# A state space stage in a two-layer trunk: response matrices on SyncE's queue, and half of the output projection in seven products

## The chip, the core and the metric

The kernel runs on one core of one Trainium2 chip. The core has five engines with instruction streams of their own: TensorE (PE, matrix products into PSUM; PEld is its weight load), VectorE (DVE), ScalarE (ACT), GpSimd (POOL) and SyncE (SP, which here only issues DMAs). Sixteen DMA engines move data between HBM and SBUF for all of them. The metric is the device time of one execution in microseconds (us); lower is better.

## What is computed

The reference is a trunk of two layers on 256 tokens of width 2048, all in float32: layer 0 mixes tokens with a gated MLP, layer 1 with a state space layer; each then has a cross-attention over 256 memory rows and a squared-ReLU MLP. The change lies in the state space layer, whose reference is, cut to its core:

```python
def s5_glu(h, w_in, lam_re, lam_im, log_dt, bm_re, bm_im, cm_re, cm_im, d_skip, w_out, b_out):
    u = (h @ w_in).astype(F32).reshape(bsz, seq, B_GROUPS, B_GROUP)
    ...
    _, states = lax.associative_scan(combine, (a, bu), axis=0)
    y = jnp.einsum('gcp,sbgp->bsgc', cmat, states).real + d_skip.astype(F32) * u
    y = jax.nn.gelu(y.reshape(bsz, seq, B_WIDTH), approximate=False).astype(h.dtype)
    val, gate = jnp.split(y @ w_out + b_out, 2, axis=-1)
    return val * jax.nn.sigmoid(gate)
```

There are 128 groups of 16 channels with 64 complex states each. `w_in` is 2048 x 2048, `w_out` 2048 x 4096.

## The kernel before

**Products in float32.** PE multiplies a reduced form of float32. Every operand is therefore split into a high part (a cast, on ACT, L103) and a low part (source minus high part, on DVE, L104), and a product is high x high, low x high and high x low. A weight tile is 128 x 1024 (two k tiles of 128 rows by 512 columns, 512 KB). SP loads it (`wload`, L117 to L128, four raw buffers), `wtile` splits it (three buffers of each part), and `gemm_tok` (L141) lets PE run 12 matmuls on it: two k tiles, two halves of the tokens, three parts. After each weight tile `tick` (L83) counts one step, and `at(delay, fn)` (L78) plans other work so many steps later: this is how the small steps of the state space stage are laid between weight tiles.

**The order of instructions.** The program is traced in this order, and a scheduler at build time keeps an order by priority for each engine, in which an instruction can come later than it was traced when its buffer is not yet free. `issue_after(ins)` forces what is issued in its block behind `ins` on the same engine. `self.fed` is the last weight load. SP's DMAs are issued in order; a DMA that waits for its buffer holds up what follows it on SP.

**Seven products.** `gemm_seven` (L784) computes two column chunks at once. On the first 4 of 16 k tiles it treats tokens (two halves), k (two blocks of two k tiles) and the two chunks as 2 x 2 blocks and forms the product with seven block products instead of eight (a Winograd form). For this it takes sums of the left operand, made once (`token_sums`, L748), and differences of the raw weight tiles, made on DVE (L856, L862, L869, L876). Each block product is a split and six matmuls. The other 12 k tiles run as direct weight tiles (`direct`, L831). Four raw tiles are loaded by `fetch` (L796). Column chunks are `n0` and `n0 + 1`. Partial sums are handed to `gather`, the last ones to `end`. It runs in the attention (values, output projection) and in the second MLP.

**The state space stage** (`s5`, L1259). It has four chunks n of 32 groups. `gemm_tok` on `b_w_in` gives the chunk's inputs (8 weight tiles, so 8 steps); `follow(n)` (L1412) then plans the chunk's own steps: `inputs` (transposes), `own` (products with pq), `states`, `carry` (the recurrence on DVE), `outputs` in two halves (steps 14 and 16, with exceptions in the last chunks; L1384 multiplies with the response matrix dq, L1392 with qq), `activated` (Gelu) and `features`. Behind the four chunks stands the output projection `b_w_out`, value chunks 0 to 3 and gate chunks 4 to 7 of 512 columns, 8 weight tiles each; j = 0 begins before the last chunk's outputs are done and runs over chunks 0, 1 and 4 in turns.

**Where dq, pq and qq come from.** They were written to HBM earlier (Pd, Qd, Kd). `fetch` (L1281) loads them for a chunk, four of each:
- pq, 512 KB, on POOL's queue, four buffers;
- qq, 512 KB, on SP's queue behind `self.fed` (`stream=True`), four buffers;
- dq, the response matrix, into four fixed tiles `resp` (L1276) of 128 x 1024, lower block triangular: four pieces of 32 rows with 256, 512, 768 and 1024 values in a row (32, 64, 96 and 128 KB), on POOL's queue. The source of a piece is the pattern `[[P, 2], [(2 * T - 1) * P, 16], [1, 2 * (h + 1) * P]]` (L1293): 2 by 16 rows. A piece for chunk n can land only when the outputs of chunk n - 1 have read the tile.

`load` (L1269) chooses the queue. In `follow`, dq of a chunk n > 0 is planned at steps 7 and 9 (8 and 10 for the last chunk), qq at 10 and 12 (11 and 13), two at a time; for chunk 0 dq is issued at the start and qq at steps 2, 4, 6 and 8. The preparation of the stage during the first MLP loads lb with SP, whose sources have the patterns [8][16][512] (L1165, L1166).

**Closing of a chunk pair** (L1467 to L1483): value and gate accumulators get their bias (loaded on POOL), sigmoid on ACT, product, residual add, all on 128 x 1024, and one step later the next norm's chunk.

Of the kernel before, what the change touches and what calls it, by code (L numbers as in the profile page):

```python
# [9 lines left out]
F32 = mybir.dt.float32  # L10
F32R = mybir.dt.float32r
I32 = mybir.dt.int32
AF = mybir.ActivationFunctionType
ALU = mybir.AluOpType
AX = mybir.AxisListType

P = 128
D = 2048
S = 256
KT = D // P  # L20
NB = 512
NCH = D // NB
KB = 2
# [15 lines left out]
class Trunk:  # L39
# [741 lines left out]
                    made.add(k)  # L781
        return raw, t1, t2, load, add

    def gemm_seven(self, tiles, token, sums, w, n0, k0, gather, end=None, own=None, ahead=None, then=None, raw=None):  # L784

# [2 lines left out]
        nc = self.nc  # L790
        v = nc.vector
        kc0 = k0 // KB
        ws, run, kept = tiles
        raw, half = raw or {}, lambda t: t.rearrange("p (k c) -> p k c", k=KB)

        def fetch(i, j):  # L796
            t = ws()
            self.fed = nc.sync.dma_start(out=half(t), in_=w[n0 + j, kc0 + i]).ins
            raw[i, j] = t

        def parts(src, own=None):
# [6 lines left out]
        def into(key, kts, left, hi, lo):  # L808
            out = banks[key]
            mm = lambda s, m, e: nc.tensor.matmul(out, s, m, start=key not in begun, stop=e, skip_group_check=True)  # L810
            for kk in kts:
                ah, al = left(kk)
                mm(ah, hi[:, kk, :], False)
                begun.add(key)
                mm(al, hi[:, kk, :], False)
            for kk in kts:
                mm(left(kk)[0], lo[:, kk, :], True)
# [13 lines left out]
        def direct(j, first):  # L831

            kc = todo[j].pop(0)
            hi, lo = self.wtile(w, n0 + j, kc0 + kc)
            for t in (first, 1 - first):
                into((t, j), range(KB), lambda kk: token(KB * kc + kk, t), hi, lo)
                yield
            self.tick()

        def whole(*a):  # L840
            for _ in direct(*a):
                pass
# [8 lines left out]
        for i, j in ((0, 0), (0, 1), (1, 0), (1, 1)):  # L851
            if (i, j) not in raw:
                fetch(i, j)
        run = run()
# [32 lines left out]
        while len(todo[0]) > 1 or len(todo[1]) > 1:  # L887
            j = len(todo[1]) > len(todo[0])
# [370 lines left out]
    def s5(self, x, cur, nxt):  # L1259
        nc, a, tc = self.nc, self.a, self.tc  # L1260
        hT = cur.act
        NQ = G // NCH
        with tc.tile_pool(name="s5", bufs=2, reuse_waits="tile") as sp:
            yT = self.new_act()
            st = {}

            ahead = {}

            def load(src, out, stream=False):  # L1269
                if stream:  # L1270
                    with tc.issue_after(self.fed):
                        nc.sync.dma_start(out=out, in_=src)
                else:
                    nc.gpsimd.dma_start(out=out, in_=src)

            resp = [sp.tile([P, T * P], F32, name=f"dq{i}", bufs=1) for i in range(4)]  # L1276
# [4 lines left out]
            def fetch(nm, n, i, stream=False):  # L1281


                if nm == "pq":
                    t = sp.tile([P, 2, 4, P], F32, name=nm, bufs=4)
                    load(self.Pd[4 * n + i], t, stream)
                elif nm == "qq":
                    t = sp.tile([P, 2, 4 * P], F32, name=nm, bufs=4)
                    load(self.Qd[4 * n + i].rearrange("l p r n -> (l p) r n"), t, stream)
                else:  # L1290
                    t, kd = resp[i], self.Kd[4 * n + i]
                    for h in range(4):
                        load(bass.AP(tensor=kd.tensor, offset=kd.offset + 6 * P,  # L1293
                                     ap=[[P, 2], [(2 * T - 1) * P, 16], [1, 2 * (h + 1) * P]]),
                             t[32 * h:32 * h + 32, 2 * (3 - h) * P:])
                ahead[nm, n, i] = t

            def chunks(n, acc):
# [17 lines left out]
            def inputs(n):  # L1316
                u = st[n].pop()
                us = sp.tile([P, 8, 4, NC], F32, name="us")
                st[n] += [us]
                for h in range(2):  # L1320
                    pt = self.ps([P, 4, P])
                    for l in range(4):
                        nc.tensor.transpose(pt[:, l, :], u[:, 4 * h + l].rearrange("p j c -> p (j c)"), self.ident)
                    nc.scalar.copy(out=us[:, 4 * h:4 * h + 4].rearrange("p l t c -> p l (t c)"), in_=pt)
# [87 lines left out]
            def follow(n):  # L1412

                late = n == NCH - 1
                self.at(5 + late, lambda: own(n))
                for i in range(4):
                    if n + 1 < NCH:
                        self.at(5, lambda i=i: fetch("pq", n + 1, i))
                    if n:
                        self.at(7 + late + i // 2 * 2, lambda i=i: fetch("dq", n, i))  # L1420
                        self.at(10 + late + i // 2 * 2, lambda i=i: fetch("qq", n, i, True))
                self.at(4 + late, lambda: inputs(n))
                self.at(6 + late, lambda: states(n))
                self.at(7 + late, lambda: [carry(n, 2, 15), carry(n, 4, 7, 2)])
                self.at(8 + late, lambda: [carry(n, c, 1, 4) for c in (8, 12, 16)])
                self.at(9 + late, lambda: [carry(n, c, 1, 4) for c in (20, 24, 28)])
                self.at(10 + late, lambda: [carry(n, 6, 7, 2), carry(n, 3, 15)])
                gap = n == NCH - 2
                self.at(14 + 1.5 * gap, lambda: outputs(n, 0))
                self.at(16 + gap, lambda: outputs(n, 1))  # L1430
                self.at(16 + gap, lambda: activated(n))
                self.at(17 + gap if n >= NCH - 2 else 19, lambda: features(n))

            for i in range(4):
                fetch("pq", 0, i)
            for i in range(4):
                fetch("dq", 0, i)
                self.at(2 * i + 2, lambda i=i: fetch("qq", 0, i, True))
            for n in range(NCH):
                acc = self.gemm_tok(hT, a["b_w_in"], n)  # L1440
                if n == 0:
# [1 line left out]
                chunks(n, acc)  # L1443
                follow(n)

            nxt.start()
            wo = a["b_w_out"]
            for j in range(NCH):
                if j == 0:
                    spare = self.psM.pop()  # L1450
                    av1 = [spare.tile([P, NB], F32, name="ps") for _ in range(2)]
                    part = lambda n, acc, k: self.gemm_tok(yT, wo, n, acc=acc, kts=range(*k), first=k[0] == 0,
                                                           last=k[1] == KT)
                    av, _, ag = (part(n, acc, (0, 4)) for n, acc in ((0, None), (1, av1), (NCH, None)))
                    for k in (4, 8):
                        for n, acc in ((0, av), (1, av1), (NCH, ag)):
                            part(n, acc, (k, k + 4))
                    self.flush()
                    for n, acc in ((0, av), (NCH, ag)):
                        part(n, acc, (12, KT))  # L1460
                elif j == 1:
                    av = part(1, av1, (12, KT))
                    ag = self.gemm_tok(yT, wo, NCH + 1)
                else:
                    av = self.gemm_tok(yT, wo, j)
                    ag = self.gemm_tok(yT, wo, NCH + j)
                cs = slice(j * NB, (j + 1) * NB)  # L1467
                bv = self.bc(sp, a["b_b_out"][j * NB:(j + 1) * NB])
                bg = self.bc(sp, a["b_b_out"][D + j * NB:D + (j + 1) * NB])
                val = sp.tile([P, 2, NB], F32, name="val", tag="pq", bufs=4)  # L1470
                gat = sp.tile([P, 2, NB], F32, name="gat", tag="pq", bufs=4)
                b2 = lambda b: b.unsqueeze(1).broadcast_to([P, 2, NB])
                if j == 1:
                    for t in range(2):
                        nc.vector.tensor_tensor(out=val[:, t], in0=av1[t], in1=bv, op=ALU.add)
                    self.psM.append(spare)
                else:
                    nc.vector.tensor_tensor(out=val, in0=av, in1=b2(bv), op=ALU.add)
                nc.vector.tensor_tensor(out=gat, in0=ag, in1=b2(bg), op=ALU.add)
                nc.scalar.activation(out=gat, in_=gat, func=AF.Sigmoid)  # L1480
                nc.vector.tensor_tensor(out=val, in0=val, in1=gat, op=ALU.mult)
                nc.vector.tensor_tensor(out=x[:, :, cs], in0=x[:, :, cs], in1=val, op=ALU.add)
                self.at(1, lambda j=j: nxt.chunk(x, j))  # L1483
# [185 lines left out]
```

## Time and profile before

| | |
|---|---|
| median of 3 runs | 2770.2 us (2769.85 to 2771.99) |
| profiled execution | 2772.35 us, span of its instructions 2770.2 us |
| mean granted TensorE clock | 0.999 |
| PE busy | 99% of the span, 14966 matmuls |
| DVE, ACT, POOL busy | 75%, 51%, 7% |
| state space stage | about 1385 us to 1694 us after the span's start |

The profile is one execution. Busy time of PE counts matmuls, which are pipelined, so a matmul's duration is longer than its distance to the next one. A row of the timeline has the start, the duration, engine, line, operation, output and inputs, and in brackets the idle time before it and what ended it. A row of the waits has who waited for whom, then total us, times, longest. A row of the DMA issues has the queue's engine, the count, KB of one and the median time from issue to landing. A row of the table by stretches has the stretch, its length, busy time and count of instructions for PE, PEld, DVE, ACT and POOL, then granted clock, busy share of the 16 DMA engines and GB/s.

### The profile page before, as it was taken

Reading aid. Unit: us, or ns where it says so; the run is one execution under the profiler, and the core shown is the slowest. Engines: PE = TensorE matmul, PEld = TensorE weight load, DVE = VectorE, ACT = ScalarE, POOL = GpSimd, SP = SyncE. Lnnn points to the kernel's source line nnn. Section 1 sums busy time; section 2 is a strip of 40 time slices with the busy share of each in tenths; the row PEclk is TensorE's granted clock in tenths of the full one; section 3 lists DMA queues with packets and bytes.
Section 4 is the critical chain, followed back from the end, with each engine's and each line's share of the span. In section 5 each row is a group of like instructions: output and inputs, shape, how many; then the busy total and the mean of one; then the engine's idle time right before and its main releaser. Section 6 shows DMA issues by size and latency. Waiting matters only on the chain. (4 is left out here: it accounts for less than half of the span.)

```text
span 2770.2 us, 39500 instructions
## 1 busy us (share of the span) xinstructions
PE 2748.3 (99%) x14966; PEld 2325.4 (84%) x14966; DVE 2066.9 (75%) x2835; ACT 1426.7 (51%) x1822; POOL 184.9 (7%) x331
## 2 busy tenths in 40 slices
PE   9999999999999999999999999999999999999998
PEld 7888888888888888888888788888888888888887
DVE  6865757878888878787577657568767978879685
ACT  5545545655544434444566445446555655546454
POOL 0100000001011111111203100000000000000000
PEclk9999999999999999999999999999999999999999
DMA  8766566457688887886879766564556557575565
GB/s 293 231 199 214 189 193 217 152 160 238 211 281 259 262 258 257 265 259 219 235 239 284 207 203 206 188 213 156 181 165 231 180 171 241 158 246 166 176 212 160
DMA packets 194175, 593.75 MB, mean 214 GB/s; under 512 B 44096, under 2 KB 45168, under 8 KB 193472
## 3 DMA queue, kind: packets, MB, share of 16 engines
q1 hardware_dynamic: 153456, 537.46, 61.1%
q0 software_dynamic: 40000, 52.71, 6.6%
q8 instruction: 117, 1.92, 0.3%
q10 hardware_dynamic: 528, 1.06, 0.1%
q14 instruction: 74, 0.61, 0.1%
HBM read 567.51 MB, written 23.46 MB: 213 GB/s over the span
## 5 line engine op out<-in xcount | busy, mean ns | idle before, releaser
L104 DVE TENSOR_TENSOR wlo<-wraw,whi 128x1024 fp32r<-128x1024 f32 (+1 forms) x857 | 1041.0, 1220 | 434.8 <-ACT whi L103 429.0
L103 ACT CAST whi<-wraw 128x1024 fp32r<-128x1024 f32 (+1 forms) x857 | 899.4, 1051 | 800.2 <-PE acc L910 172.1
L174 PE MATMUL acc<-act,whi 128*128 128x512 f32 x3072 | 740.9, 391 | 0.6 <-DVE act L246 0.6
L174 PEld LDWEIGHTS acc<-act,whi 128*128 128x128 f32 x3072 | 563.1, 188 | 110.6 <-issue 1.4
L179 PEld LDWEIGHTS acc<-act,wlo 128*128 128x128 f32 x3072 | 395.0, 191 | 17.4 <-DVE wlo L104 1.8
L179 PE MATMUL acc<-act,wlo 128*128 128x256 f32 x3072 | 403.3, 283 | 1.3 <-DVE wlo L104 1.0
L159 PE MATMUL acc<-whi,act 128*128 128x512 f32 x1472 | 370.4, 393 | 5.6 <-ACT whi L103 5.5
L159 PEld LDWEIGHTS acc<-whi,act 128*128 128x128 f32 x1472 | 275.2, 189 | 63.6 <-ACT whi L103 6.3
L810 PE MATMUL acc<-whi,act 128*128 128x512 f32 x824 | 222.7, 392 | 0.0
L910 PE MATMUL acc<-whi,hl 128*128 128x512 f32 x544 | 212.7, 391 | 0.0
L909 PE MATMUL acc<-whi,hh 128*128 128x512 f32 x544 | 212.6, 391 | 0.0
L159 PE MATMUL acc<-wlo,act 128*128 128x512 f32 x736 | 197.9, 391 | 0.0
L810 PEld LDWEIGHTS acc<-whi,act 128*128 128x128 f32 x824 | 152.9, 188 | 35.9 <-ACT ends L846 2.2
L159 PEld LDWEIGHTS acc<-wlo,act 128*128 128x128 f32 x736 | 138.6, 188 | 28.9
L912 PE MATMUL acc<-wlo,hh 128*128 128x512 f32 x544 | 145.8, 389 | 0.0
L810 PE MATMUL acc<-wlo,act 128*128 128x512 f32 x412 | 127.2, 391 | 0.2
L190 ACT COPY r<-acc 128x512 f32<-128x512 f32 x64 | 37.6, 587 | 161.9 <-PE acc L174 161.9
L910 PEld LDWEIGHTS acc<-whi,hl 128*128 128x128 f32 x544 | 102.1, 188 | 22.2 <-issue 1.0
L810 PE MATMUL acc<-whi,hh 128*128 128x512 f32 x308 | 120.5, 391 | 0.0
L909 PEld LDWEIGHTS acc<-whi,hh 128*128 128x128 f32 x544 | 102.1, 188 | 21.4 <-issue 0.2
L912 PEld LDWEIGHTS acc<-wlo,hh 128*128 128x128 f32 x544 | 102.0, 188 | 21.4 <-issue 0.2
L810 PE MATMUL acc<-whi,hl 128*128 128x512 f32 x308 | 119.9, 389 | 0.0
(387 smaller groups left out, 2951.3 us busy)
## 6 DMA issues: line engine op xcount, KB each, us to landing
wraw<-in_f_w_up SPq DMA_DIRECT2D x256, 512.0 KB, 4.5
wraw<-in_f_w_down SPq DMA_DIRECT2D x200, 512.0 KB, 5.6
wraw<-in_x_w_q SPq DMA_DIRECT2D x64, 512.0 KB, 3.7
wraw<-in_x_w_k SPq DMA_DIRECT2D x64, 512.0 KB, 4.5
wraw<-in_b_w_out SPq DMA_DIRECT2D x64, 512.0 KB, 4.5
wraw<-in_a_w_in SPq DMA_DIRECT2D x63, 512.0 KB, 4.7
wraw<-in_x_w_o SPq DMA_DIRECT2D x48, 512.0 KB, 4.3
wraw<-in_x_w_v SPq DMA_DIRECT2D x40, 512.0 KB, 3.9
```

Source lines behind the costliest of these rows:

```text
L103: self.nc.scalar.copy(out=hi, in_=src)
L104: return self.nc.vector.tensor_tensor(out=lo, in0=src, in1=hi.bitcast(F32), op=ALU.subtract).ins
L159: nc.tensor.matmul(out[t], a[:, kt, sl], b[:, kk, :], start=st and a is ah, stop=en)
L174: nc.tensor.matmul(acc[:, f, :], hi[:, kk, sl], both[:, kt].rearrange("p a s -> p (a s)"), start=first and kk == 0, stop=last and kk == FK ...
L179: nc.tensor.matmul(acc[:, f, 0:S], lo[:, kk, sl], ah[:, kt, :], start=False, stop=last and kk == FK - 1, skip_group_check=True)
L190: nc.scalar.copy(out=dst, in_=acc[:, :, S:])
L810: mm = lambda s, m, e: nc.tensor.matmul(out, s, m, start=key not in begun, stop=e, skip_group_check=True)
L909: nc.tensor.matmul(acc[:, t, :], ah, hi[:, kk, :], start=kt == 0, stop=False)
L910: nc.tensor.matmul(acc[:, t, :], al, hi[:, kk, :], start=False, stop=False)
L912: nc.tensor.matmul(acc[:, t, :], hid[kt // 4][0][:, kt % 4, sl], lo[:, kk, :], start=False, stop=kt == KT - 1)
```

## The change

1. `load` takes the queue for dq too, and dq is loaded on SP's queue behind `self.fed`, with its steps moved: for chunk 0 at steps 6, 8, 14 and 16 (qq three steps after each), for the others at 12, 12, 14 and 14, and qq one step after. Pieces and tiles stay as they are.
2. Value chunks 2 and 3 run with their gate chunks 6 and 7 through `gemm_seven`, with a distance `step=NCH` between the two column chunks. The sums of yT are made once, three steps into j = 1. Raw tiles live in the four `resp` tiles, the kept partial sums in tiles of the stage that are free by then.
3. With `step > 1`, `fetch` in `gemm_seven` issues the raw tiles behind the last weight load.
4. The closing of these two pairs runs by halves of the tokens: bias adds, sigmoid, product and residual add on 128 x 512.

```diff
-    def gemm_seven(self, tiles, token, sums, w, n0, k0, gather, end=None, own=None, ahead=None, then=None, raw=None):
+    def gemm_seven(self, tiles, token, sums, w, n0, k0, gather, end=None, own=None, step=1, ahead=None, then=None, raw=None):
...
             t = ws()
-            self.fed = nc.sync.dma_start(out=half(t), in_=w[n0 + j, kc0 + i]).ins
+            with self.tc.issue_after(self.fed) if step > 1 else nullcontext():
+                self.fed = nc.sync.dma_start(out=half(t), in_=w[n0 + step * j, kc0 + i]).ins
             raw[i, j] = t
...
-            hi, lo = self.wtile(w, n0 + j, kc0 + kc)
+            hi, lo = self.wtile(w, n0 + step * j, kc0 + kc)
...
                     for h in range(4):
-                        load(bass.AP(tensor=kd.tensor, offset=kd.offset + 6 * P,
+                        load(stream=stream, src=bass.AP(tensor=kd.tensor, offset=kd.offset + 6 * P,
                                      ap=[[P, 2], [(2 * T - 1) * P, 16], [1, 2 * (h + 1) * P]]),
-                             t[32 * h:32 * h + 32, 2 * (3 - h) * P:])
+                             out=t[32 * h:32 * h + 32, 2 * (3 - h) * P:])
...
-                    if n:
-                        self.at(7 + late + i // 2 * 2, lambda i=i: fetch("dq", n, i))
-                        self.at(10 + late + i // 2 * 2, lambda i=i: fetch("qq", n, i, True))
+                for k, nm in enumerate(("dq", "qq")) if n else ():
+                    for i in range(4):
+                        self.at(12 + i // 2 * 2 + k, lambda nm=nm, i=i: fetch(nm, n, i, True))
...
-            for i in range(4):
-                fetch("dq", 0, i)
-                self.at(2 * i + 2, lambda i=i: fetch("qq", 0, i, True))
+            for k, nm in enumerate(("dq", "qq")):
+                for i in range(4):
+                    self.at((6, 8, 14, 16)[i] + 3 * k, lambda nm=nm, i=i: fetch(nm, 0, i, True))
...
+            def block_sums():
+                y = sp.tile([P, 4, S], F32, name="ysum", tag="qq", bufs=4)
+                nc.vector.tensor_tensor(out=y, in0=yT[0][:, 0:4].bitcast(F32), in1=yT[1][:, 0:4].bitcast(F32), op=ALU.add)
+                sums.append(self.token_sums(sp.tile([P, KB * NB], F32, name="s", tag="qq", bufs=4),
+                                            lambda: sp.tile([P, 4, 2, P], F32R, name="sums", tag="us"),
+                                            y[:, 0:2], y[:, 2:4]))
+
+            def gated_pair(j):
+
+                cs = slice(j * NB, (j + 1) * NB)
+                bias = [self.bc(sp, a["b_b_out"][o + j * NB:o + (j + 1) * NB]) for o in (0, D)]
+                val = sp.tile([P, 2, NB], F32, name="val", tag="pq", bufs=4)
+                gat = sp.tile([P, 2, NB], F32, name="gat", tag="pq", bufs=4)
+                held, done = {}, set()
+                v = nc.vector
+
+                def part(t, n, p):
+                    v.tensor_tensor(out=p, in0=p, in1=bias[n - j], op=ALU.add)
+                    held[t, n - j] = p
+
+                def end(t, n, src):
+                    out = (val, gat)[n - j][:, t]
+                    v.tensor_tensor(out=out, in0=src, in1=held.get((t, n - j), bias[n - j]), op=ALU.add)
+                    if n > j:
+                        nc.scalar.activation(out=out, in_=out, func=AF.Sigmoid)
+                    done.add((t, n - j))
+                    if (t, 0) in done and (t, 1) in done:
+                        v.tensor_tensor(out=val[:, t], in0=val[:, t], in1=gat[:, t], op=ALU.mult)
+                        v.tensor_tensor(out=x[:, t, cs], in0=x[:, t, cs], in1=val[:, t], op=ALU.add)
+
+                run = sp.tile([P, KB * NB], F32, name="run", tag="u", bufs=1)
+                keep = [sp.tile([P, 2, NB], F32, name="keep", tag="vv") for _ in range(2)]
+                homes = iter(resp)
+                self.gemm_seven((lambda: next(homes), lambda: run, lambda i: keep[i // 2][:, i % 2]),
+                                lambda kt, t: [f[:, kt, t * P:(t + 1) * P] for f in yT[:2]],
+                                sums, wo, j, 0, part, end, step=NCH)
...
+            sums = []
             for j in range(NCH):
+                if j == 1:
+                    self.at(3, block_sums)
+                if j >= 2:
+                    gated_pair(j)
+                    self.at(1, lambda j=j: nxt.chunk(x, j))
+                    continue
```

More of the change, by code (lines that the diff above doesn't have):

```diff
@@ L1460, in s5 @@
                         part(n, acc, (12, KT))
-                elif j == 1:
+                else:
                     av = part(1, av1, (12, KT))
                     ag = self.gemm_tok(yT, wo, NCH + 1)
-                else:
-                    av = self.gemm_tok(yT, wo, j)
-                    ag = self.gemm_tok(yT, wo, NCH + j)
                 cs = slice(j * NB, (j + 1) * NB)
```

## The prediction

> **What bounds the kernel now.** I read the page first, then the PE's waits, then the state space stage on PE, POOL and SyncE (SP), then the DMA issues. On the page (the row of q1, the queue of SP, has packets, MB moved and the share of 16 engines' span) and in the list of PE's waits:
>
> ```profile
> span 2770.2 us, 39500 instructions
> PE 2748.3 (99%) x14966; PEld 2325.4 (84%) x14966; DVE 2066.9 (75%) x2835; ACT 1426.7 (51%) x1822; POOL 184.9 (7%) x331
> q1 hardware_dynamic: 153456, 537.46, 61.1%
> ```
> ```profile
> PE acc L159 <- ACT whi L103: 5.5, 1, 5.5
> PE ps L1384 <- DMA dq<-Kd: 2.5, 2, 1.9
> PE ps L1337 <- ACT us L1324: 1.7, 2, 0.9
> ```
>
> PE is busy 99% of the span, and its few waits add up to about 12 us. So there are two ways to gain: fewer matmuls, or the 2.5 us that the last chunk's outputs wait for response matrices. There is more room to lose: whatever starves PE of split weight tiles goes straight into the time. The stage on PE, first the start of the first half of the outputs of chunks 0 and 3, then the two halves of chunk 3 with the tiles beside them:
>
> ```profile
> 1453.38 1.08 PE L1384 MATMUL ps<-dq,us 128*32 128x128 f32 x32
> ...
> 1545.07 1.07 PE L159 MATMUL acc<-wlo,act 128*128 128x512 f32 x4
> 1546.06 1.08 PE L1384 MATMUL ps<-dq,us 128*32 128x128 f32 x32
> ...
> 1551.07 1.98 PE L159 MATMUL ps<-whi,act 128*128 128x512 f32 x8
> 1552.88 1.07 PE L159 MATMUL ps<-wlo,act 128*128 128x512 f32 x4
> 1554.56 0.65 PE L1384 MATMUL ps<-dq,us 128*32 128x128 f32 x16 [0.61 <-DMA dq<-Kd]
> 1557.06 0.80 PE L1384 MATMUL ps<-dq,us 128*32 128x128 f32 x16 [1.85 <-DMA dq<-Kd]
> 1557.79 1.96 PE L1392 MATMUL ps<-qq,vv 64*32 64x128 f32 x64
> 1559.68 2.63 PE L159 MATMUL acc<-whi,act 128*128 128x512 f32 x8
> ...
> 1563.06 1.04 PE L1407 MATMUL ps<-ident,y 128*128 128x128 f32 x8
> ```
>
> From the second half of a weight tile, over one half of the outputs, to the end of the next tile takes 1545.07 to 1551.07, 6.0 us, and in the stalled pass 1552.88 to 1563.06, 10.2 us. The wait of 2.5 us costs 4.2 us, because the granted clock is at 0.50 behind it (stretches of the span; the last three numbers of a row are granted clock, DMA share and GB/s):
>
> ```profile
> 745.20:746.70 1.50, 1.50 (x10) 1.28 (x9) 1.50 (x3) 0.62 (x1) 0.00 (x0) 1.00 0.34 53
> 1385.00:1400.00 15.00, 15.00 (x72) 12.42 (x70) 11.33 (x29) 8.42 (x14) 0.00 (x0) 1.00 0.87 319
> 1558.00:1560.00 2.00, 2.00 (x65) 1.61 (x54) 0.00 (x0) 0.20 (x1) 0.00 (x0) 0.50 0.18 70
> 1590.00:1695.00 105.00, 105.00 (x472) 86.85 (x471) 58.67 (x55) 47.80 (x56) 2.15 (x4) 1.00 0.67 200
> ```
>
> **The change, part 1: seven products.** A direct weight tile (12 matmuls) against two products (6 each) of the function that the second layer's output projection already runs:
>
> ```profile
> 1569.39 1.98 PE L159 MATMUL acc<-whi,act 128*128 128x512 f32 x8
> ...
> 1572.11 1.98 PE L159 MATMUL acc<-whi,act 128*128 128x512 f32 x8
> ```
> ```profile
> 2020.72 1.07 PE L810 MATMUL acc<-whi,act 128*128 128x512 f32 x4
> ...
> 2022.08 1.07 PE L810 MATMUL acc<-whi,act 128*128 128x512 f32 x4
> ```
>
> A tile takes 2.72 us (1569.39 to 1572.11), a product 1.36 us (2020.72 to 2022.08). Each pair of chunks drops one product of eight on 4 of 16 k tiles, so two pairs save 12 matmuls, 2 x 1.36 = 2.7 us. New beside them are, per pair, three more splits and four differences on DVE, and once the sums of yT (four small operations, an add and a split). DVE is busy 58.7 and ACT 47.8 of 105 us in the stretch that they enter (last window row), so PE's weight tiles hide them; without that cover the sums would cost their own few microseconds of DVE, once. The two pairs' raw tiles all live in the four response tiles, free since the outputs of chunk 3, 30 us before the first pair; I cost their entry at nothing, as in the same function's passes above, which list no wait. Halving the closing operations (adds, sigmoid, product by halves) shortens the tail to the next norm, which hides behind the attention's first tiles: nothing either.
>
> **Part 2: the response matrices.** The DMA issues, with KB of one and us from issue to landing, POOL's issues of chunk 3, and SP's around chunk 1:
>
> ```profile
> pq<-Pd POOLq DMA_DIRECT2D x16, 512.0 KB, 7.8
> qq<-Qd SPq DMA_DIRECT2D x16, 512.0 KB, 10.8
> dq<-Kd POOLq DMA_DIRECT2D x16, 128.0 KB, 11.8
> dq<-Kd POOLq DMA_DIRECT2D x16, 96.0 KB, 13.8
> dq<-Kd POOLq DMA_DIRECT2D x16, 64.0 KB, 13.7
> dq<-Kd POOLq DMA_DIRECT2D x16, 32.0 KB, 13.0
> ```
> ```profile
> 1525.05 4.70 POOL L1274 DMA_DIRECT2D dq<-Kd  x8 [6.41 <-PE ps L1384]
> ...
> 1545.10 0.59 POOL L1274 DMA_DIRECT2D dq<-Kd  x1 [2.22 <-DMA dq<-Kd]
> ```
> ```profile
> 1395.74 59.51 SPq L127 DMA_DIRECT2D wraw<-in_b_w_in  x20
> 1455.36 1.23 SPq L1272 DMA_DIRECT2D qq<-Qd  x2
> ```
>
> One matrix is four pieces, 32 + 64 + 96 + 128 = 320 KB; a chunk has four, 1280 KB (1.31 MB). Small as they are, they land later than a 512 KB transfer of the same queue. Chunk 3's sixteen went out from 1525.05, and the last let PE go at 1557.06: 1.31 MB in 32.0 us, 41 GB/s. One of the 16 engines moves 537.46 MB / (0.611 x 16 x 2770.2 us) = 19.8 GB/s. A stream of pieces therefore runs as if on two engines. Their source has an outermost dimension of 2 (L1294), where weights, pq and qq have 128 rows. On SP's own queue there is a likeness: the loads of lb, outermost dimension 8 (L1165, L1166). Two were issued 0.67 us apart, with a weight tile before them, and in the stretch behind them the engines are busy 0.34 (first window row), not 0.87 as in the second:
>
> ```profile
> 743.34 0.35 SPq L127 DMA_DIRECT2D wraw<-in_f_w_down  x1
> 743.80 0.62 SPq L1168 DMA_DIRECT2D lb<-in_b_pc  x1
> 744.47 0.69 SPq L1168 DMA_DIRECT2D lb<-Ld  x1
> ```
>
> Had the second load taken the eight engines that the first leaves free, the share would be near one. So I take it that SP's narrow loads use the same engines each time, and that all pieces will land on one pair of engines. Each weight tile, spread over all 16, is complete only when its part on that pair is, and that part stands behind the pieces in the same queue.
>
> The Trainium skill, "DMA: Bandwidth & Descriptors", section "Why a DMA increments its semaphore by 16 and not by 1", says that a copy runs on the largest number up to 16 that divides the outermost sizes of both its sides, and on SP's and ACT's queues always on the lowest-numbered engines. By that rule the pieces (2 and 32) use the same two engines, and the sum is the one below; the 41 GB/s agree with two, and no row here shows which two.
>
> The sum for that pair: at 19.8 GB/s (all of q1) a 512 KB transfer takes 32768 B / 19.8 = 1.65 us of each engine, a matrix 163840 B / 19.8 = 8.25 us of each of the two. At 319 GB/s / (0.87 x 16) = 22.9 GB/s (second window row) it is 1.43 and 7.15, at 70 / (0.18 x 16) = 24.3 (third row) 1.35 and 6.74.
> - From 1453.38 to 1559.68 (chunk 0's first outputs to the tile behind chunk 3's last) PE now takes 106.3 us and passes 26 weight tiles. The pair must carry 26 weight tiles, 12 qq, 4 pq and 12 matrices: 42 x 1.65 + 12 x 8.25 = 168 us, or 146 us, or 138 us at the three rates. Weights run ahead by about six tiles (four raw and three split buffers), so 8 to 10 us of it can be put off once: 158, 137 or 130. PE is late by 52, 31 or 23 us. The stall of 4.2 us is inside the 106.3, so its removal is counted.
> - Before that, from 1385, 68.4 us: 22 weight tiles, 4 qq, 8 pq and 4 matrices are 34 x 1.65 + 4 x 8.25 = 89 us, or 77 us; less the same lead, 0 to 11 us late.
>
> Together 23 to 63 us. I take 50, above the middle, since PE's clock halves behind each stall and the pair also stands idle when SP waits for a response tile to be read. The ends stay in the range. Moved with the pieces are the 16 qq loads, already on SP, now one step behind; what queues behind a waiting SP is every weight tile, and PE waits for those. POOL keeps only pq, at no cost.
>
> The profiled execution took 2772.35 us, its span 2770.2, and the median is 2770.2, so differences are put on the median: 2770.2 - 2.7 + 50 = 2817.5, about 2818 us. This measurement can tell about 0.2%, 5.5 us, from no change.
>
> **The rivals.**
> 1. The pieces take different engines each time, or all of them. For it: POOL's pieces come no faster than 41 GB/s and yet cost PE only one stall. Against it: the 0.34. Then they land in time and the stall goes: 2770.2 - 2.7 - 4.2 = 2763 us, faster. The Trainium skill's first page, "Trainium Kernel Development and Optimization", section "Key Constraints", says that the queues of SP, ACT and POOL run on the same 16 engines and that issuing from several only saves issue time; by that rule the move itself changes nothing, and this is the time. The 61.1% of q1 agree with shared engines only in that no engine is full now.
> 2. The same, but each of six bursts of eight pieces (two matrices, 16.5 us of a pair) uses up the lead of six tiles (6 x 2.72 = 16.3 us) on some engine, about 1 us each: 2769 us, no difference.
> 3. Spread pieces, but SP stands at a piece until PE has read the response tile, weights behind it. It decides where that wait exceeds the lead left; at 5 us for each of chunks 1 to 3, 2763 + 15 = 2778 us, slower. Against it: the pieces stand 12 and 14 steps after their chunk, six steps after the read that frees the tile, about SP's lead.
>
> **How the numbers follow.** Forecast 0.80, rival 1 0.13, rival 2 0.05, rival 3 0.02. Faster 0.13, same 0.05, slower 0.82. The forecast's own range is 2770.2 - 2.7 + 23 = 2790 to 2770.2 - 2.7 + 63 = 2830, and above that six bursts with 1.7 us of slow clock each (4.2 - 2.5) and 15 us of a standing pair: 2856. With a little for rates beyond the rows, 2860; downward to 2775, which takes in rival 3 and leaves out rivals 1 and 2.
>
> **What would show it.** Right: PE waits for splits of wraw in 1400 to 1600 that end on the DMA of in_b_w_in and in_b_w_out, most of all behind pieces; a low DMA share, not a high one, in those stretches; clock dips; the last outputs of chunk 3 near 1600 rather than 1557. The matmuls drop by 12, to 14954, and the last two chunk pairs take 2.7 us less. Wrong: no wait on wraw, dq landing in under 8 us from SP, a high DMA share; then rival 1 holds. If the stage keeps its length and the pairs gain nothing, DVE has become late in the products' first tiles.

## The result and the profile after

The changed kernel takes 2841.67 us (median of 5 runs, 2840.68 to 2844.77) against 2769.85 us before in the same session (5 runs): 1.0263 times as long, 95% interval 1.0248 to 1.0278. It is 72 us slower; the forecast, 2818, was 48 us above the kernel before (50 lost, 2.7 gained).

The page after, and PE's waits:

```profile
span 2839.7 us, 39556 instructions
PE 2760.4 (97%) x14954; PEld 2329.7 (82%) x14954; DVE 2090.2 (74%) x2871; ACT 1435.9 (51%) x1839; POOL 146.8 (5%) x267
q1 hardware_dynamic: 155632, 542.71, 59.9%
```
```profile
PE ps L159 <- ACT whi L103: 15.1, 1, 15.1
PE ps L1338 <- ACT us L1325: 14.1, 3, 12.4
PE ps L1354 <- ACT z L1342: 13.4, 1, 13.4
PE acc L159 <- ACT whi L103: 11.1, 4, 5.4
```

The matmuls fell by 12, but PE's list of waits adds up to some 68 us, where it was about 12. The rest is in PE's busy time, 2760.4 us after 2748.3 with 12 matmuls fewer: the clock, below. No wait ends on dq any more. All four rows name ACT, a cast or a small copy, and neither is the cause. ACT's own timeline shows it:

```profile
1497.05 1.09 ACT L1325 COPY us<-ps 128x512 f32<-128x512 f32 x2
1518.08 1.04 ACT L103 CAST whi<-wraw 128x1024 fp32r<-128x1024 f32 x1 [19.93 <-DMA wraw<-in_b_w_in]
1519.03 1.19 ACT L1342 COPY z<-ps 128x256 f32<-128x256 f32 x4
```

ACT stands 19.93 us at the cast of a weight tile that has not landed. The copy of z, which PE waits for, is queued behind that cast. So the releaser that the list names is one step short of the cause, a late weight load. PE's side, the first and last outputs, and the matmuls that stood:

```profile
1469.45 1.08 PE L1385 MATMUL ps<-dq,us 128*32 128x128 f32 x32
...
1519.72 1.97 PE L1354 MATMUL ps<-ident,z 128*128 128x128 f32 x8 [13.38 <-ACT z L1342]
...
1617.95 3.78 PE L159 MATMUL ps<-whi,act 128*128 128x512 f32 x8 [15.06 <-ACT whi L103]
...
1626.19 1.08 PE L1385 MATMUL ps<-dq,us 128*32 128x128 f32 x32
...
1628.34 2.12 PE L159 MATMUL acc<-whi,act 128*128 128x512 f32 x8
```

The first row stood at 1453.38 before, the last at 1559.68: PE is 16.1 us late at the first and 68.7 us late at the last, and the span grew by 69.5. The whole loss lies in this stage, 16 us ahead of chunk 0's outputs and 52.6 us from there to the tile behind chunk 3's. Four stretches of it (length, busy PE, PEld, DVE, ACT, POOL, then granted clock, DMA share, GB/s):

```profile
1385.00:1453.00 68.00, 58.85 (x313) 46.59 (x313) 34.53 (x67) 30.72 (x56) 2.11 (x4) 0.97 0.71 210
1486.00:1494.00 8.00, 6.76 (x37) 5.41 (x36) 6.06 (x12) 3.78 (x10) 0.00 (x0) 1.00 0.14 55
1505.00:1560.00 55.00, 32.73 (x254) 26.20 (x253) 25.11 (x59) 18.16 (x36) 0.00 (x0) 0.77 0.62 186
1560.00:1625.00 65.00, 41.61 (x484) 33.55 (x485) 27.84 (x58) 19.59 (x27) 0.00 (x0) 0.77 0.53 151
```

The second row is a share of 0.14, 2.2 of 16 engines, while pieces are being moved. The last two show the clock at 0.77 in stretches where PE is busy 60% and 64% of the time. SP's issues and the DMA rate in 40 equal slices of 1465 to 1530:

```profile
1470.15 5.26 SPq L1273 DMA_DIRECT2D dq<-Kd  x8
1475.52 1.80 SPq L127 DMA_DIRECT2D wraw<-in_b_w_in  x1
...
1483.39 12.42 SPq L1273 DMA_DIRECT2D dq<-Kd  x8
```
```profile
GB/s 229 214 408 403 416 202 52 67 260 250 281 279 228 60 50 53 58 50 48 51 72 245 247 330 314 345 331 330 343 305 325 136 53 55 118 275 50 242 110 47
```

The rate alternates between about 50 GB/s (two engines) and 250 to 400 (most of them). A weight tile leaves one completion record for each engine. Read from the trace's records, in us after the issue:

```
issued    tile    parts 1 to 14     parts 15 and 16
1475.52   wraw    5.16 to 5.91      15.47, 15.61
1477.41   qq      5.21 to 5.95      14.84, 14.97
1482.56   wraw    3.50 to 4.77      12.24, 12.36
1495.91   wraw    5.41 to 6.58      22.08, 22.09
```

Fourteen of the sixteen parts of a tile are there after 4 to 7 us, and the last two come 8 to 16 us later. The last row is the tile for which ACT stood 19.93 us: it is complete at 1518.00, and the cast starts at 1518.08. Eight pieces went out ahead of the tiles of 1475.52 and of 1495.91; had they used different engines, more than two parts would be late. This is the pair of the forecast, seen directly. The Trainium skill, "DMA: Bandwidth & Descriptors", section "Why a DMA increments its semaphore by 16 and not by 1", has SP's narrow copies on the lowest-numbered engines each time, and GpSimd's on consecutive engines that move round from copy to copy; the first half agrees with these records (two late parts, every time), though they do not tell which numbers the two have. No record here shows the second half directly.

### The profile page after: what moved, and what is told of

Read it like the earlier page. It is cut to its first block, busy times and chain, and to the rows that moved or that the text cites. A ratio compares the mean times of both kernels' runs of the same rounds, so it can differ in the third digit from the quotient of the medians.

```text
span 2839.7 us, 39556 instructions
## 1 busy us (share of the span) xinstructions
PE 2760.4 (97%) x14954; PEld 2329.7 (82%) x14954; DVE 2090.2 (74%) x2871; ACT 1435.9 (51%) x1839; POOL 146.8 (5%) x267
## 3 DMA queue, kind: packets, MB, share of 16 engines
q10 hardware_dynamic: 528, 1.06, 0.1%
## 5 line engine op out<-in xcount | busy, mean ns | idle before, releaser
L159 PEld LDWEIGHTS acc<-wlo,act 128*128 128x128 f32 x608 | 115.2, 190 | 25.3 <-DVE wlo L104 1.0
```

The lines of the kernel that those rows point to most:

```text
L159: nc.tensor.matmul(out[t], a[:, kt, sl], b[:, kk, :], start=st and a is ah, stop=en)
```

## The experiments

Each is compared with the kernel before on the same chip; the ratio is followed by its 95% interval.

**One part alone.** `e1_seven_alone` is the changed kernel with the two loading plans of before, so pieces on GpSimd's (POOL's) queue:

```diff
-                        self.at(12 + i // 2 * 2 + k, lambda nm=nm, i=i: fetch(nm, n, i, True))
+                        self.at(7 + late + i // 2 * 2, lambda i=i: fetch("dq", n, i))
+                        self.at(10 + late + i // 2 * 2, lambda i=i: fetch("qq", n, i, True))
```

> The kernel after with the queue and the steps of dq and qq put back as before; the seven products stay. Theory (the narrow pieces on SP's queue pile up on one pair of DMA engines): about 2767 us, the 2.7 us of 12 matmuls below before, and the wait of 2.5 us for dq in the last chunk still there. Rival A (the pieces hold SP's queue up by their number, their issue time and their waits for the response tile, whatever engines carry them): the same 2767. Rival B (a good part of the loss comes from the seven products, whose splits and differences starve PE): 2780 or more.

Measured: 2769.81 us, ratio 1.0001 (0.9991 to 1.0012). No gain, against the 2.7 us of the theory. `e2_move_alone` is the kernel before with only the queue and the steps changed (the same lines the other way round).

> The kernel before with only the queue and the steps of dq and qq as after; no seven products. Theory and rival A: the whole loss and the 2.7 us that the products save, about 2844 us. Rival B: clearly less, 2830 or below.

Measured: 2842.79 us, ratio 1.0268 (1.0252 to 1.0284). The move, queue and steps together, is the whole loss.

**Queue or steps.** `e8_late_steps_pool` keeps the changed steps and puts the pieces back on POOL's queue:

```diff
-  fetch(nm, n, i, True)
+  fetch(nm, n, i, nm == "qq")
```

> The changed kernel with the response matrices' pieces, at the changed steps, back on GpSimd's queue. Theory (the loss is SP's queue, not the later steps): no wait for wraw of over 3 us in the state space stage; PE waits for dq a little longer than before, since the pieces go out later, 2768 to 2785 us. Rival (the later steps are what makes them late): 2800 us or more, with PE waiting for dq.

Measured: 2769.56 us, ratio 0.9998 (0.9989 to 1.0008). Against the changed kernel nothing but the queue of the 64 pieces is edited, and 72 us are gone. PE's wait for dq is 1.1 us, where a little more than the 2.5 us of before was expected. Its weight tile issued at 1464.67 has its sixteen parts between 4.95 and 8.71 us, with no pair behind the rest.

**Bytes or issues.** `e9_quarter` leaves queue, steps and 64 issues, and makes each piece a quarter as wide (the response tiles are zeroed as a whole first):

```diff
-  ap=[[P, 2], [(2 * T - 1) * P, 16], [1, 2 * (h + 1) * P]]
+  ap=[[P, 2], [(2 * T - 1) * P, 16], [1, (h + 1) * P // 2]]
```

> The changed kernel with its 64 pieces a quarter as wide: same queue, steps, number of issues and outermost dimension 2, a quarter of the bytes. The other three quarters of the response matrices stay zero, so that part of the chunks' outputs is left out. Theory (bytes on two engines are the larger cost): a matrix now takes 2.06 us of each of the two, 42 x 1.65 + 12 x 2.06 = 94 us, less 8 to 10 of lead 84 to 86, against PE's 106: what stays is SP's issue time, bursts of eight x 0.45 to 0.65 us = 4 to 5 us, twice in four steps beside four qq, mostly under the lead of 16 us: 2768 to 2785 us. Rival (the place in SP's order costs it, whatever the bytes): 2830 us or more.

Measured: 2765.9 us, ratio 0.9988 (0.9979 to 0.9997), a little below what the theory gave. PE's waits from 1385 to 1660 are a single row:

```profile
PE ps L1323 <- ACT u L1312: 0.4, 1, 0.4
```

64 issues on SP, the order among the weights and the reads of the response tiles are all still there, and cost nothing. What costs 76 us is the other three quarters of the bytes, on two engines. One reservation: the scheduler's order differs from the changed kernel's in seven places on ACT and two on DVE (it is that of `e8_late_steps_pool`). `e10_quarter_cut`, below, bears on it: its order is the changed kernel's except for one cast on ACT, and with light transfers it takes 2776.46 us. So that order alone does not cost 76 us.

**Cutting the pieces for all engines.** `e3_pieces_cut` splits each piece into two of 16 rows, outermost dimension 16, so 128 issues; `e4_half_cut` does that for every second matrix.

```diff
-  ap=[[P, 2], [(2 * T - 1) * P, 16], [1, 2 * (h + 1) * P]]   # once for each h
+  ap=[[(2 * T - 1) * P, 16], [1, 2 * (h + 1) * P]]           # for g in range(2), offset (6 + g) * P
```

> The kernel after with each piece of a response matrix loaded as two transfers of 16 rows, so that the outermost dimension of the source is 16 and no longer 2; same bytes, same queue, same steps, 128 instead of 64 issues on SP. Theory: the pieces spread over the 16 engines, the loss goes, 2763 to 2768 us, and PE no longer waits behind casts of b_w_in or b_w_out. Rival A: no better than 2842, rather worse with twice the issues.

> As with all pieces cut, but only for two of a chunk's four matrices; the other two stay as narrow pieces. Theory: the pair's load falls by half of the matrices; by the sum at 24.3 GB/s from chunk 0's to chunk 3's outputs 42 x 1.35 + 6 x 6.74 + 6 x 0.84 = 102 us against 106 us of PE, so the loss is nearly gone: 2763 to 2785. A loss simply in proportion to the narrow pieces would give about 2803. Rival A: 2842 or more.

Measured: 2802.23 us, ratio 1.0119 (1.0105 to 1.0133), and 2802.61 us, ratio 1.0121 (1.0108 to 1.0135). Both miss, and so does rival A: in `e3_pieces_cut` the pair is gone (the weight tile of 1480.06 has all sixteen parts between 3.11 and 3.85 us), and yet 33 us of the loss stay. In `e4_half_cut` the last two parts still come 3.4 to 6.1 us after the others in four weight tiles issued from 1387 to 1414. Its time is the 2803 of a loss in proportion to the narrow pieces, but with no narrow piece at all the time is the same, so it does not speak for that. I first put the 33 us down to SP's issue time, since a burst of sixteen pieces occupies SP for 7 to 12 us. `e10_quarter_cut` has the same 128 issues with a quarter of the bytes.

> The cut pieces (128 transfers of 16 rows, outermost dimension 16) a quarter as wide: the issues of the cut pieces with a quarter of their bytes, the rest of the response matrices zero as in the run with 64 quarters. Theory (the 33 us that the cut pieces still lost are SP's issue time, 7 to 12 us for a burst of sixteen): nearly the same time as the cut pieces, 2790 to 2803 us. Rival (their bytes, behind which the weight tiles stand): 2765 to 2780 us.

Measured: 2776.46 us, ratio 1.0023 (1.0013 to 1.0032). That theory fell: with the same 128 issues most of the 33 us are gone. Against `e9_quarter` it is 2776.5 - 2765.9 = 10.6 us, in which the 64 more issues, the spread over more engines and some places in the order of ACT and DVE stand together. The profile of `e3_pieces_cut` shows another cause of a part. ACT and DVE, then the DMA rate from 1395 to 1415:

```profile
1397.53 1.05 ACT L103 CAST whi<-wraw 128x1024 fp32r<-128x1024 f32 x1 [1.67 <-PE acc L159]
1407.53 1.22 ACT L1314 ACTIVATE u<-acc,rstd 32x128 f32<-32x128 f32 x4 [8.95 <-DVE u L1311]
```
```profile
1406.59 0.84 DVE L1311 TENSOR_TENSOR u<-acc,rstd 32x256 f32<-32x256 f32 x2 [6.75 <-PE acc L159]
```
```profile
GB/s 106 188 385 418 410 418 385 410 410 434 401 385 418 426 442 418 205 0 0 0 0 0 0 0 0 0 0 0 0 0 0 0 0 0 147 147 336 336 123 57
```

For 8 us no byte moves: ACT waits for the end of a chunk's accumulation with the casts of landed weight tiles queued behind it, so no raw buffer comes free and SP stands. In the changed kernel's build these casts stand ahead of the activation. Laid beside the changed kernel's, the sequence of instructions of this kernel differs in some 10 places on PE, 12 on ACT and 40 on DVE (that of `e4_half_cut` in 9, 16 and 31), while that of the quarter-wide cut differs in none on PE and DVE and two on ACT: with other transfers the scheduler at build time chose another order. At the first outputs of chunk 0 PE is already 14 us behind in it (1467.3 against 1453.4 before), and not at all in the quarter-wide cut (1452.7). The two cuts lie 26 us apart; how much of that is order and how much bytes, no run separates.

**One wide load for a matrix.** `e5_one_load_sp` fetches each matrix by one transfer on SP, zeros included, outermost dimension 8:

```diff
-  four pieces: ap=[[P, 2], [(2 * T - 1) * P, 16], [1, 2 * (h + 1) * P]]
+  one: offset=kd.offset, ap=[[P, 8], [(2 * T - 1) * P, 16], [1, T * P]], out=t
```

> The changed kernel with each response matrix fetched by one transfer (outermost dimension 8, 512 KB with the zeros, 16 issues in all) in place of four pieces of two; queue and steps as changed. Theory (the pieces cost two things: two engines carry all of them, and the cut pieces showed that SP spends 7 to 12 us on a burst of sixteen issues, with the weight tiles behind it): eight engines carry 12 matrices x 64 KB / 19.8 GB/s = 3.3 us each, 40 us beside 42 x 1.65 = 69 us, together 109 less 8 to 10 of lead, against PE's 106: both costs are gone, 2763 to 2772 us. Rival (SP stands at a response tile until PE has read it, whatever the transfers look like): the loss of the cut pieces stays, 2795 to 2805 us.

Measured: 2802.41 us, ratio 1.0111 (1.0096 to 1.0125). The number is the rival's, the mechanism is not: SP issues two loads in 1.4 us and goes on. The order of instructions on PE, ACT and DVE is that of `e9_quarter`, so here it is the transfers. PE's waits in the stage, and the rate from 1465 to 1530:

```profile
PE ps L1336 <- ACT us L1323: 16.1, 2, 9.9
PE ps L159 <- ACT whi L103: 5.8, 1, 5.8
PE ps L1322 <- ACT u L1311: 3.4, 1, 3.4
```
```profile
GB/s 222 171 182 171 169 187 176 350 310 408 209 179 179 141 199 164 108 192 214 204 308 378 398 408 418 303 257 179 217 212 212 224 219 242 270 413 239 207 237 174
```

Where the pair gave 50 GB/s, there are now stretches of 170 to 220: eight engines. The weight tile issued at 1461.93 has eight parts at 6.14 to 7.07 us and eight at 15.58 to 15.91. The expectation's own sum (109 us of the eight engines against PE's 106) had no margin but the lead, and the lead can be spent once, while three chunks each bring a burst.

**The wide load on POOL's queue**, with the seven products (`e6_one_load_pool`) and in the kernel before (`e7_before_one_load`):

> Seven products, with the response matrices on GpSimd's queue at the steps of the kernel before, each fetched by one transfer (outermost dimension 8, 512 KB). Theory (the stalls for dq in that queue come from two engines' width): no wait of PE for dq in chunk 3, 2.5 us of wait and 1.7 us of slow clock less: 2763 to 2768 us. Rival (the wider transfers and their 60% more bytes delay the weights on the shared engines): waits for wraw, 2773 us or more.

> The kernel before with one transfer for each response matrix, nothing else. Theory: as the run with the seven products on GpSimd's queue, 0 to 3 us above it (what the seven products are worth when nothing waits for dq): 2765 to 2769 us. Rival (they are worth nothing, since the next wait, for the memory's chunks, takes it back): the same time within 1 us.

Measured: 2785.49 us, ratio 1.0055 (1.0042 to 1.0068), and 2779.39 us, ratio 1.0032 (1.002 to 1.0045). Both theories miss, and so does the second's rival; the first's holds. The 6 us between the two, with the seven products the slower, were expected by no case, and no run explains them. The stall for dq is gone from the second, whose order on PE, ACT and DVE is that of the kernel before, and a longer wait stands in its place. The first row is from its waits in the stage, the second is ACT ahead of the longer of the two, held by a late weight tile, and the two others are the stretch from 1453 to 1505 in the kernel before and in this one:

```profile
PE ps L1335 <- ACT us L1322: 10.0, 2, 6.0
```
```profile
1483.96 1.04 ACT L103 CAST whi<-wraw 128x1024 fp32r<-128x1024 f32 x1 [6.79 <-DMA wraw<-in_b_w_in]
```
```profile
1453.00:1505.00 52.00, 51.13 (x642) 41.52 (x641) 40.35 (x104) 32.47 (x64) 18.19 (x31) 1.00 1.02 297
```
```profile
1453.00:1505.00 52.00, 46.02 (x612) 37.44 (x612) 34.75 (x80) 27.42 (x52) 6.95 (x12) 0.97 1.02 285
```

The engines' share (packets' times, which can overlap) is at 1.02 in this stretch of the kernel before already, and with 60% more bytes of response matrices the weights come late. That the engines had no room left is argued from this share; other stretches moved over 400 GB/s, where this one moved 297.

**The seven products and their raw tiles.** `e12_pool_late_no_seven` is the kernel before with the changed steps, pieces on POOL's queue; `e11_pool_not_held` is `e8_late_steps_pool` without the block that holds the raw tiles back.

> The kernel before with the response matrices and qq at the changed steps, the pieces on GpSimd's queue as before, and no seven products. Theory (the later steps cost nothing there, and the seven products' 12 matmuls are taken back by the wait for the memory's chunks): the same as before and as the run with seven products, 2767 to 2772 us. Rival (the seven products are worth their 2.7 us once the steps are later): 2 to 3 us above the run with them, 2771 to 2773 us.

Measured: 2768.03 us, ratio 0.9997 (0.9988 to 1.0006), against 2769.56 with the seven products: they are worth nothing here.

```diff
-            with self.tc.issue_after(self.fed) if step > 1 else nullcontext():
+            with nullcontext():
```

> The changed kernel with the pieces back on GpSimd's queue at the changed steps, and the raw tiles of the seven products not held back behind the tile ahead of them. Theory (the holding back only orders SP's queue, and no transfer is late there): the same as with holding back within 3 us, 2766 to 2773 us. Rival (raw tiles issued early stand ahead of the direct weight tiles): PE waits on whi in the last two pairs, 2775 us or more.

Measured: 2774.81 us, ratio 1.0017 (1.0008 to 1.0026), 5.2 us above the same kernel with holding back; the theory's range is missed, and so is the rival's wait on whi. The first raw tile now goes out before chunk 3's last response matrix has landed, and PE waits for that (SP, then PE, then POOL's last issue of a piece):

```profile
1546.78 0.33 SPq L799 DMA_DIRECT2D dq<-in_b_w_out  x1
```
```profile
1558.58 0.89 PE L1385 MATMUL ps<-dq,us 128*32 128x128 f32 x16 [4.06 <-DMA dq<-Kd]
```
```profile
1542.81 0.59 POOL L1275 DMA_DIRECT2D dq<-Kd  x1 [3.39 <-DMA dq<-Kd]
```

In the kernel that holds back, the four raw tiles go out at 1584.84, and the waits for dq add up to 1.1 us. But the raw tile is not shown to be the cause. The last piece lands at 1558.45 against 1554.08 there, 4.4 us later, and 3.6 us of that were already there when POOL issued it (1542.81 against 1539.17), before the raw tile went out. Where the 5.2 us come from stays open.

No version beat the kernel before by more than the 0.2% that can be told; the quarter-wide pieces, which leave work out, are 0.12% below it.

## Why the prediction was right, and what was mis-sized

**The mechanism was right.** SP's narrow pieces share one pair of engines every time, and a weight tile is complete only when its two parts behind them are. The completion records show it, `e9_quarter` removes the loss by taking bytes from the pair, and `e8_late_steps_pool` by taking the queue. Rivals 1 to 3, all of them with spread pieces, are out. With rival 1 falls, for this kernel, the rule of the Trainium skill's first page, "Trainium Kernel Development and Optimization", section "Key Constraints", by which issuing from several queues saves issue time alone: the queue of 64 transfers decided 72 us. The 0.34 of the lb loads, taken from a stretch 700 us earlier, was the row that told. One sign that the prediction took for two engines was none: the 41 GB/s of POOL's pieces. POOL issued each of the last five of chunk 3 just after the piece eight issues before it had landed (the last at 1545.10 after 1544.81), and from 1525 to 1557 its pieces took 20.4% of 16 engines' time, 3.3 engines and not two.

**The sum of the pair was mis-sized.** I had three rates for one engine, 19.8, 22.9 and 24.3 GB/s, and took 50 us, above the middle of 23 to 63.
- Main stretch: 52, 31 or 23 us late were worked out; 52.6 were measured, what the slowest rate gives, but by two errors that cancel. The first is the rate. In the row of 1486 to 1494, where hardly anything else moves, the pair makes 55 / (0.14 x 16) = 24.6 GB/s each. By the completion records it has parts outstanding through three bursts, 1473.24 to 1524.32, 1527.90 to 1573.52 and 1581.46 to 1623.07, together 138.3 us, in which 12 matrices, 12 qq, 4 pq and 16 weight tiles pass. That is 12 x 160 KB + 32 x 32 KB = 3.01 MB of either engine, about 21.8 GB/s. At this rate the whole load, 42 x 32 KB + 12 x 160 KB = 3.34 MB, takes 153 us, and PE took 1628.34 - 1469.45 = 158.9 us for the stretch. The second error is the lead, 8 to 10 us that the sum took off. It was not gained: SP issued 27 weight tiles in the stretch for the 26 that PE passed, so no lead was spent between its two ends. At 19.8 GB/s the load is 15 us too long, and the lead takes most of that back. That the slowest rate fits is luck.
- Ahead of it: 0 to 11 us worked out, 16.1 measured. Here too, 21.8 GB/s and no lead come nearer: 34 x 32 KB + 4 x 160 KB take 81 us, 13 more than PE's 68.4. What is left of both stretches, 6 and 3 us, no run takes apart; standing queues and the low clock (0.97 in the first) are in it.

**The seven products' 2.7 us were not kept.** In the kernel before the first tile of the attention starts at 1694.65 (first fence, PE; second, ACT); with the seven products alone (third fence, PE; fourth, ACT) at 1692.76, 1.9 us earlier, and then it stands:

```profile
1694.65 1.98 PE L174 MATMUL acc<-act,whi 128*128 128x512 f32 x8
...
1726.74 1.21 PE L179 MATMUL acc<-act,wlo 128*128 128x256 f32 x8 [0.25 <-DVE wlo L104]
```
```profile
1706.63 2.11 ACT L254 ACTIVATE act<-memc,gcol 128x256 fp32r<-128x256 f32 x5 [1.46 <-DMA memc<-in_mem_t]
1708.65 0.56 ACT L190 COPY z<-acc 128x512 f32<-128x512 f32 x1
1709.11 1.05 ACT L103 CAST whi<-wraw 128x1024 fp32r<-128x1024 f32 x1
```
```profile
1692.76 1.98 PE L174 MATMUL acc<-act,whi 128*128 128x512 f32 x8
...
1713.18 2.88 PE L174 MATMUL acc<-act,whi 128*128 128x512 f32 x8 [2.51 <-ACT whi L103]
...
1729.41 1.21 PE L179 MATMUL acc<-act,wlo 128*128 128x256 f32 x8 [0.29 <-DVE wlo L104]
```
```profile
1706.95 1.71 ACT L254 ACTIVATE act<-memc,gcol 128x256 fp32r<-128x256 f32 x4 [3.90 <-DMA memc<-in_mem_t]
1710.41 1.30 ACT L254 ACTIVATE act<-memc,gcol 128x256 fp32r<-128x256 f32 x3 [1.75 <-DMA memc<-in_mem_t]
1711.62 0.56 ACT L190 COPY z<-acc 128x512 f32<-128x512 f32 x1
1712.08 1.99 ACT L103 CAST whi<-wraw 128x1024 fp32r<-128x1024 f32 x2
```

ACT stands at the memory's chunks, with the casts that PE needs behind them. In the kernel before five chunks stand ahead of the next cast, which starts at 1709.11; with the seven products it is seven, and the cast starts at 1712.08. The kernel before waits for no cast at this place, and with the seven products PE leaves it 2.7 us later than before (1729.41 against 1726.74). The same is seen in a second pair of profiles, `e8_late_steps_pool` against `e12_pool_late_no_seven`: 1.2 us ahead at the attention's first tile, 0.9 us behind after a wait of 1.06 us for whi at 1719.01. My step "hides behind the attention's first tiles: nothing either" looked at DVE's and ACT's busy time and not at what is queued on ACT there. The size is uncertain: the profiled execution of `e1_seven_alone` took 2775.1 us, the longest of its eleven, and over the runs the two kernels cannot be told apart.

**The signature held in part.** Waits on casts that end on DMAs of b_w_in and b_w_out, 12 matmuls fewer, clock dips and the shift of chunk 3 came as named (its last outputs at 1626.19, not near 1600). The low DMA share was right for the time ahead of a wait (0.14) and wrong for the wait itself, where queued weights and pq run on the other engines (0.62 from 1505 to 1560). The 2.7 us of the last two pairs were wrong in the sum, since PE loses them right behind these pairs.

## What to carry to other kernels

Before a transfer is moved to another queue, look at how many engines its shape gives it there, and whether they are the same each time; then sum bytes for the busiest engine, not for all sixteen, and use the rate that those engines hold through a whole burst (21.8 GB/s here), not that of a quiet moment (24.6). Take off a lead only if the stretch ends with it spent. Put narrow transfers where no wide one that others wait for stands behind them. When a wait names a small copy on an in-order engine, read what stands ahead of it in that engine's queue.

## What the runs showed that was not expected

- POOL's pieces are not cheap, only spread. From 1525 to 1557 of the kernel before, bytes and share of both queues:

```profile
q1 hardware_dynamic: 1846, 6.71, 72.8%
q0 software_dynamic: 2563, 1.33, 20.4%
```

  POOL's 1.33 MB take 0.204 x 16 x 32 = 104 us of engine time, 12.7 GB/s for each engine, and SP's 6.71 MB 18.0 GB/s. So they take engine time from the weights, but no run shows one pair that carries them all.
- Late landings hold SP's issues up too. In the changed kernel the eight pieces issued from 1483.39 to 1494.94 take SP 12.42 us: each goes out 0.02 to 0.07 us after the landing of the transfer eight issues before it (1487.36 after 1487.35, 1489.88 after 1489.87). A weight tile behind narrow pieces is therefore late twice, issued late and completed late. `e9_quarter`, with as many issues, has no such loss.
- `e10_quarter_cut` takes 10.6 us longer than `e9_quarter`; the 64 extra issues are one of several differences between them.
- Changing only the shape of transfers changed the build's order of instructions on three engines, and in one place let all DMA engines idle for 8 us (`e3_pieces_cut`). A run meant to change one thing had changed two.
